# The last expert's way back to its tokens: two d-tiles in turns, two quarters, and a product on GpSimd

## The chip, the core and the metric

The kernel runs on one core of one Trainium2 chip. The metric is the device time of one execution in microseconds, as the median of several runs. TensorE is called PE here, VectorE DVE, ScalarE ACT, GpSimd POOL and SyncE SP.

## What is computed

A decoder trunk of two layers over 512 tokens of width 1024: an mLSTM mixer and a dense SwiGLU, then an HGRN2 mixer and a top-2-of-8 expert SwiGLU. Only the end matters here:

```python
def moe_swiglu(h, router_w, wg, wu, wd):
    ...
    for e in range(N_EXPERTS):
        y = y + gates[:, e:e + 1] * swiglu(t, wg[e], wu[e], wd[e])
    ...
        x = x + gate2 * y
    return rmsnorm(x, final_norm_w)
```

The final norm needs the sum of squares of each token's whole row, so no output row is ready before the last expert's whole row has been added.

## The kernel before

**Work and order.** Every expert gets up to 152 of the tokens (`CAP`). Weights are cut into blocks of 128 x 128; eight blocks are a slot. For every slot, ACT rounds the raw slot to a high half (`whi`) and DVE subtracts that to get the low half (`wlo`); there are five buffers of each, so the high half of a slot can be made only when PE is through with the slot five before it. A block is two matmuls (`mm2`): the high half against both halves of the activations (304 columns), the low half against the high half (152 columns). All engines run strictly in the order in which the program issues; the order is written by hand.

`Weights.get` (lines 254 to 275) is called for every block. Where a block is the first of a slot s, it issues, in this order, the low half of slot s+2 on DVE, the high half of slot s+3 on ACT, then the tasks that are due at s, and only then come the slot's matmuls. `W.at(n, f)` makes f due n slots later; `W.flush` issues all that is left.

**The experts** (`experts`, lines 1597 to 1786). An expert has eleven gate-and-up steps of 16 blocks (`act` makes the hidden activations `hb` from each in five tasks, one slot apart) and a down product of eight d-tiles of eleven blocks (f = 0 to 10, one for each hidden tile). For the last expert the down product is the last thing that PE streams. Before it `W.flush` issues the tasks of the last hidden tiles at once. `down` (lines 1678 to 1722) treats a finished d-tile in tasks: b0 scales one half out of PSUM (ACT), b1 adds the other (DVE, two instructions), b2 transposes the result (PE), and at every fourth d-tile b3 copies the four transposed tiles out. They are due one, two, three and four slots later:

```python
            for i, g in enumerate((b0, b1, b2) + ((b3,) if dd == 3 else ())):
                W.at(i + 1, g)
```

The last expert's first half (d-tiles 0 to 3) goes to memory (`YL`) by two DMAs from POOL (lines 1718 and 1719). Its second half (d-tiles 4 to 7) stays on the chip as four tiles of high and low halves (`last_y`). `add` fetches the rows of the earlier experts for 128 tokens by an indirect DMA from POOL and adds them on DVE (`xt<-yg`), three and four slots later.

**The finish** (`finish`, lines 1798 to 1833). POOL gathers `YL` for four groups of 128 tokens (`yl`). DVE adds each to the residual `xt` and multiplies by the norm's weights (`o<-xt,fw`), ACT sums the squares. Then for each group PE spreads the second half over the tokens by four matmuls with the selection matrix `sel` (`la`, 512 columns), DVE adds, ACT squares; DVE computes 1/sqrt in eight small instructions for two groups at a time (`fv`, `fsy`, `fsa`), DVE and ACT scale the row, and SP sends it out:

```python
            f0(0), f0(1), f0(2), f1(0), f0(3), f2(0), f2(1), f1(1), f2(2), f2(3)
```

Of the kernel before, what the change touches and what calls it, by code (L numbers as in the profile page):

```python
# [21 lines left out]
P = 128  # L22
D = 1024
T = 512
# [60 lines left out]


# [321 lines left out]
class Kernel:  # L408
# [1099 lines left out]
    def moe(self, out, stop):  # L1508
        nc, tc = self.nc, self.tc
        V, S = nc.vector, nc.scalar  # L1510
        with ExitStack() as ctx:
# [28 lines left out]
            g, r, n_over = self.experts(*pools, xt, pick, lambda: rest(*slots))  # L1540
            experts.close()
            self.finish(xt, g, r)
# [54 lines left out]
    def experts(self, xp, hp, wk, xt, pick, rest):  # L1597
# [80 lines left out]
        def down(e, d, yp):  # L1678
# [3 lines left out]
            final = (e, j) == (NE - 1, 1)  # L1682
# [24 lines left out]
            def b3():  # L1707
                if final:
                    for q, n in enumerate((P, R2)):
                        hi, lo = (self.xp.tile([P, T], F32R, name=f"ly{x}{q}", tag="x")[:n] for x in "hl")  # L1710
                        S.activation(hi, tp[q], AF.Copy)
                        V.tensor_sub(lo, tp[q], hi.bitcast(F32))
                        self.last_y += [(q, hi), (q, lo)]
                    return
                for q in range(2):
                    S.activation(yt[q][:, j], tp[q], AF.Copy)
                to, r0 = (self.YL, 0) if e == NE - 1 else (self.Y[j], e * CAP)
# [6 lines left out]
        self.last_y = []  # L1724
# [27 lines left out]
        for kind, e, i in moe_steps():  # L1752
# [21 lines left out]
            else:  # L1774
                if e == NE - 1 and i == 0:
                    W.flush()
                if e == NE - 1 and i in adds[1]:
                    n = len(adds[0]) + adds[1].index(i)
                    add(n % 4, n // 4)
                yp = self.ps(f"yd{e}{i}", (P, 2, CAP))  # L1780
                for f in range(ET):
                    self.mm2(yp, W.get(b), hs[e, f], f == 0, f == ET - 1)
                    b += 1
                down(e, i, yp)
        W.flush()
        return g, r, n_over
# [11 lines left out]
    def finish(self, xt, g, r):  # L1798

        nc, tc = self.nc, self.tc  # L1800
        V, S = nc.vector, nc.scalar
        with tc.tile_pool(name="fin", bufs=4) as fp:
            ssq = fp.tile([P, 2, NC], F32, name="zs", bufs=1)
            zr = fp.tile([P, NC], F32, name="zr", bufs=1)
            o = [fp.tile([P, 2, 512], F32, name=f"o{i}", tag="o") for i in range(NC)]
            ys = [self.xp.tile([P, T], F32, name=f"yl{i}", tag="x") for i in range(NC)]
            for i, y in enumerate(ys):
                nc.gpsimd.indirect_dma_start(out=y, out_offset=None, in_=self.YL,
                                             in_offset=bass.IndirectOffsetOnAxis(ap=r["last"][:, 0, i:i + 1], axis=0))
            for i, y in enumerate(ys):  # L1810
                V.scalar_tensor_tensor(xt[i][0], y, g["last"][:, 0, i:i + 1], xt[i][0], op0=OP.mult, op1=OP.add)
                S.activation(y, xt[i][0], AF.Square, accum_out=ssq[:, 0, i:i + 1])
                V.tensor_mul(o[i][:, 0], xt[i][0], self.fw[:, 0])
            V.tensor_scalar(zr, ssq[:, 0], 1.0 / D, EPS, op0=OP.mult, op1=OP.add)

            def f0(i):
                ps = self.ps(f"la{i}")
                for n, (q, y) in enumerate(self.last_y):
                    nc.tensor.matmul(ps, self.sel[q][:, i * P:(i + 1) * P], y, start=n == 0, stop=n == 3)
                V.scalar_tensor_tensor(xt[i][1], ps, g["last"][:, 0, i:i + 1], xt[i][1], op0=OP.mult, op1=OP.add)  # L1820
                S.activation(o[i][:, 1], xt[i][1], AF.Square, accum_out=ssq[:, 1, i:i + 1])

            rs = {}

            def f1(n):
                v = fp.tile([P, 2], F32, name=f"fv{n}", tag="fv")
                V.scalar_tensor_tensor(v, ssq[:, 1, 2 * n:2 * n + 2], 1.0 / D, zr[:, 2 * n:2 * n + 2], op0=OP.mult, op1=OP.add)
# [50 lines left out]
def _pack(inp):  # L1878
# [17 lines left out]
    moe = np.concatenate([gu, dn], 1).reshape(NE * MB // 8, 8, P, P).transpose(0, 2, 1, 3)  # L1896
# [35 lines left out]
```

## Time and profile before

| | us |
|---|---|
| median of three runs | 1565.17 |
| lowest and highest run | 1562.8 and 1565.18 |
| the profiled execution, device time | 1557.43 |
| its span, first to last instruction | 1555.7 |
| PE busy in the span | 1492.9 |
| DVE busy in the span | 1089.2 |
| ACT busy in the span | 845.3 |
| POOL busy in the span | 133.3 |

The profile is of one execution, which was shorter than the timed ones; times on its axis are microseconds from the start of its span. A busy PE is not a PE at its peak, since matmuls are pipelined. The views used are the page, the busy time by stretch, the timelines of single engines and the rows of one source line. Nearly every instruction is recorded under line 337, that of a helper, so operations are told by the names of what they write and read.

### The profile page before, as it was taken

Reading aid. Unit: us, or ns where it says so; the run is one execution under the profiler, and the core shown is the slowest. Engines: PE = TensorE matmul, PEld = TensorE weight load, DVE = VectorE, ACT = ScalarE, POOL = GpSimd, SP = SyncE. Lnnn points to the kernel's source line nnn. Section 1 sums busy time; section 2 is a strip of 40 time slices with the busy share of each in tenths; the row PEclk is TensorE's granted clock in tenths of the full one; section 3 lists DMA queues with packets and bytes.
Section 4 is the critical chain, followed back from the end, with each engine's and each line's share of the span. In section 5 each row is a group of like instructions: output and inputs, shape, how many; then the busy total and the mean of one; then the engine's idle time right before and its main releaser. Section 6 shows DMA issues by size and latency. Waiting matters only on the chain.

```text
span 1555.7 us, 23596 instructions
## 1 busy us (share of the span) xinstructions
PE 1492.9 (96%) x8955; PEld 1306.8 (84%) x8955; DVE 1089.2 (70%) x1991; ACT 845.3 (54%) x1561; POOL 133.3 (9%) x215
## 2 busy tenths in 40 slices
PE   4989999999999999999999999999999999999996
PEld 3867777888888888688888876899999999999994
DVE  6885774645445555595977744787878878787896
ACT  5566433422212322365656543687786868777763
POOL 0041000000000000310000020501010010101051
PEclk9999999999999999999999999999999999999997
DMA  9462551455455553543102152588687877878792
GB/s 374 167 202 75 196 191 54 156 197 200 157 183 187 193 191 120 186 152 109 55 28 82 55 187 108 194 280 301 249 284 276 277 274 256 300 251 278 275 335 91
DMA packets 80902, 300.47 MB, mean 193 GB/s; under 512 B 8084, under 2 KB 8132, under 8 KB 79760
## 3 DMA queue, kind: packets, MB, share of 16 engines
q1 hardware_dynamic: 68608, 263.21, 47.8%
q0 software_dynamic: 12176, 35.70, 6.9%
q8 instruction: 72, 1.18, 0.3%
q14 instruction: 46, 0.38, 0.1%
HBM read 280.78 MB, written 18.09 MB: 192 GB/s over the span
## 4 chain that ended last, share of the span: by engine, by line
PE 86%; DVE 7%; ACT 3%; DMA 2%; issue 2%; DVEq 0%; SPq 0%; ACTq 0%
PE gu L337 21%; PE yd L337 11%; PE fd L337 8%; PE fgp L337 7%; PE fup L337 7%; PE hh L337 4%; PE al L337 3%; PE hv L337 3%; PE h_out L337 3%; PE m_g L337 3%; PE m_out L337 2%; PE hg L337 2%; PE o L337 2%; PE v L337 1%; PE f_in L337 1%
## 5 line engine op out<-in xcount | busy, mean ns | idle before, releaser
L337 DVE TENSOR_TENSOR wlo<-raw,whi 128x1024 fp32r<-128x1024 f32 x403 | 489.7, 1222 | 101.7 <-ACT whi L337 99.8
L337 ACT ACTIVATE whi<-raw 128x1024 fp32r<-128x1024 f32 x403 | 422.1, 1055 | 169.0 <-DMA raw<-in_w 35.9
L337 PE MATMUL gu<-x,whi 128*128 128x304 f32 x1408 | 358.7, 344 | 1.4 <-DVE x L337 1.0
L337 PE MATMUL gu<-x,wlo 128*128 128x152 f32 x1408 | 327.8, 233 | 0.6 <-issue 0.6
L337 PEld LDWEIGHTS gu<-x,wlo 128*128 128x128 f32 x1408 | 269.1, 191 | 0.7 <-issue 0.4
L337 PEld LDWEIGHTS gu<-x,whi 128*128 128x128 f32 x1408 | 264.4, 188 | 1.9 <-DVE x L337 1.1
L337 PE MATMUL yd<-hb,whi 128*128 128x304 f32 x704 | 181.4, 346 | 1.3 <-DVE hb L337 1.3
L337 PE MATMUL yd<-hb,wlo 128*128 128x152 f32 x704 | 164.2, 233 | 0.0
L337 PEld LDWEIGHTS yd<-hb,wlo 128*128 128x128 f32 x704 | 134.6, 191 | 0.0
L337 PEld LDWEIGHTS yd<-hb,whi 128*128 128x128 f32 x704 | 132.3, 188 | 1.5 <-DVE hb L337 1.5
L337 DVE SCALAR_TENSOR_TENSOR ar<-ar,cond 128x1024 f32<-128x1024 f32 x80 | 98.7, 1237 | 2.8 <-DMA ar<-in_ada 2.7
L337 ACT ACTIVATE fhi<-fg 128x512 fp32r<-128x512 f32 x22 | 13.9, 633 | 114.3 <-DVE fg L337 114.3
L337 DVE TENSOR_TENSOR fg<-fg,fup 128x512 f32<-128x512 f32 x20 | 13.8, 688 | 82.7 <-PE fup L337 82.7
L337 PE MATMUL fd<-fhi,whi 128*128 128x512 f32 x176 | 69.6, 396 | 0.0
L337 PE MATMUL fd<-flo,whi 128*128 128x512 f32 x176 | 69.6, 396 | 0.0
L337 PE MATMUL fd<-fhi,wlo 128*128 128x512 f32 x176 | 69.6, 396 | 0.0
L337 ACT ACTIVATE t<-gu 128x152 f32<-128x152 f32 x176 | 48.2, 289 | 35.9 <-PE gu L337 34.3
L337 PE MATMUL fgp<-lo,whi 128*128 128x512 f32 x160 | 62.3, 389 | 0.0
L337 PE MATMUL fgp<-hi,whi 128*128 128x512 f32 x160 | 62.2, 389 | 0.0
L337 PE MATMUL fgp<-hi,wlo 128*128 128x512 f32 x160 | 62.2, 389 | 0.0
L337 PE MATMUL fup<-hi,whi 128*128 128x512 f32 x160 | 62.2, 389 | 0.0
L337 PE MATMUL fup<-lo,whi 128*128 128x512 f32 x160 | 62.2, 389 | 0.0
(410 smaller groups left out, 2990.1 us busy)
## 6 DMA issues: line engine op xcount, KB each, us to landing
raw<-in_moe SPq DMA_DIRECT2D x125, 1024.0 KB, 5.6
raw<-in_w SPq DMA_DIRECT2D x69, 1024.0 KB, 5.2
ar<-in_ada SPq DMA_DIRECT2D x80, 512.0 KB, 4.4
ad<-in_ada SPq DMA_DIRECT2D x8, 1024.0 KB, 15.2
XG<-zero POOLq DMA_DIRECT2D x18, 256.0 KB
xr<-XG POOLq DMA_DIRECT2D x28, 152.0 KB
raw<-in_moe SPq DMA_DIRECT2D x8, 512.0 KB, 3.4
Y<-yt POOLq DMA_DIRECT2D x14, 256.0 KB
```

The source lines that it names most:

```text
L337: r = f(*args, **kw)
```

## The change

- The eleven slots of the last down product are stored once more in the order `LAST`: d-tiles 0 and 1 in turns, eight blocks of each, then three of each; d-tiles 2 to 7 follow one by one.
- In the last expert every task of a d-tile is due at the next slot, in one go (b0, b1, b2 and what follows).
- The first half's gathers are issued right behind its DMAs to `YL`; the additions and squares of the first two token groups (`first`) are due four slots later.
- The second half is treated in quarters of 256 columns: the first quarter's high and low halves are made at d-tile 5, its matmuls (`share`) for groups 0 and 1 are issued behind the last block and those for 2 and 3 behind the last transposes; its additions and squares (`join`) stand in the finish, ahead of the second quarter's.
- The products with the norm's weights move from DVE to POOL.

```diff
+LAST = [(d, f) for f0, f1 in ((0, KT), (KT, ET)) for d in range(2) for f in range(f0, f1)] + \
+    [(d, f) for d in range(2, KT) for f in range(ET)]
...
-            base = (e - 1) * MB // 8 + 2 * ET
+            base = (e - 1) * MB // 8 + 2 * ET if e < NE else NE * MB // 8
...
-                    for q, n in enumerate((P, R2)):
-                        hi, lo = (self.xp.tile([P, T], F32R, name=f"ly{x}{q}", tag="x")[:n] for x in "hl")
-                        S.activation(hi, tp[q], AF.Copy)
-                        V.tensor_sub(lo, tp[q], hi.bitcast(F32))
-                        self.last_y += [(q, hi), (q, lo)]
+                    c = slice((dd - 1) * P, (dd + 1) * P)
+                    for q, n in enumerate((P, R2)):
+                        t = self.xp.tile([P, 2, 256], F32R, name=f"ly{q}{d}", tag="x")
+                        hi, lo = t[:n, 0], t[:n, 1]
+                        S.activation(hi, tp[q][:, c], AF.Copy)
+                        V.tensor_sub(lo, tp[q][:, c], hi.bitcast(F32))
+                        last_y[d // 2 - 2].extend(((q, hi), (q, lo)))
...
+                if last:
+                    for i in range(NC):
+                        t = self.xp.tile([P, T], F32, name=f"yl{i}", tag="x")
+                        nc.gpsimd.indirect_dma_start(out=t, out_offset=None, in_=self.YL,
+                                                     in_offset=bass.IndirectOffsetOnAxis(ap=r["last"][:, 0, i:i + 1], axis=0))
+                        late[i] = t
+                    for i in range(2):
+                        W.at(4, lambda i=i: first(i, late[i]))
+            def b4():
+                share(0, 2), share(0, 3)
-            for i, g in enumerate((b0, b1, b2) + ((b3,) if dd == 3 else ())):
-                W.at(i + 1, g)
+            gs = (b0, b1, b2) + ((b4,) if final and dd == 3 else ()) + ((b3,) if dd == 3 or (final and dd == 1) else ())
+            for i, task in enumerate(gs):
+                W.at(1 if last else i + 1, task)
...
+        def first(i, t):
+            V.scalar_tensor_tensor(xt[i][0], t, g["last"][:, 0, i:i + 1], xt[i][0], op0=OP.mult, op1=OP.add)
+            S.activation(t, xt[i][0], AF.Square, accum_out=self.ssq3[:, 0, i:i + 1])
+        def share(n, i):
+            if i % 2 == 0:
+                ps = self.ps(f"la{n}{i}").rearrange("p (i c) -> p i c", i=2)
+                parts_of[n, i], parts_of[n, i + 1] = ps[:, 0], ps[:, 1]
+            for m, (q, y) in enumerate(last_y[n]):
+                nc.tensor.matmul(parts_of[n, i], self.sel[q][:, i * P:(i + 1) * P], y, start=m == 0, stop=m == 3)
+        def join(n, i):
+            x = xt[i][1][:, n * 256:n * 256 + 256]
+            V.scalar_tensor_tensor(x, parts_of[n, i], g["last"][:, 0, i:i + 1], x, op0=OP.mult, op1=OP.add)
+            S.activation(late["sq"][:, :256], x, AF.Square, accum_out=self.ssq3[:, 1 + n, i:i + 1])
+        def final():
+            for i in (2, 3):
+                first(i, late[i])
+            for i in range(NC):
+                join(0, i)
+            yield
+            for i in range(NC):
+                share(1, i)
+                join(1, i)
+                yield
...
+        e, acc = NE - 1, {0: yp}
+        for d, f in LAST:
+            if d not in acc:
+                if d in adds[1]:
+                    n = len(adds[0]) + adds[1].index(d)
+                    add(n % 4, n // 4)
+                acc[d] = self.ps(f"yd{e}{d}", (P, 2, CAP))
+            self.mm2(acc[d], W.get(b), hs[e, f], f == 0, f == ET - 1)
+            b += 1
+            if f == ET - 1:
+                down(e, d, acc[d])
+        share(0, 0), share(0, 1)
         W.flush()
...
-                V.tensor_mul(o[i][:, 0], xt[i][0], self.fw[:, 0])
...
+            next(final)
+            for i in range(NC):
+                nc.gpsimd.tensor_mul(o[i][:, 0], xt[i][0], self.fw[:, 0])
+            V.tensor_add(zr, ssq[:, 0], ssq[:, 1])
+            V.tensor_scalar(zr, zr, 1.0 / D, EPS, op0=OP.mult, op1=OP.add)
...
             def f0(i):
-                ps = self.ps(f"la{i}")
-                for n, (q, y) in enumerate(self.last_y):
-                    nc.tensor.matmul(ps, self.sel[q][:, i * P:(i + 1) * P], y, start=n == 0, stop=n == 3)
-                V.scalar_tensor_tensor(xt[i][1], ps, g["last"][:, 0, i:i + 1], xt[i][1], op0=OP.mult, op1=OP.add)
-                S.activation(o[i][:, 1], xt[i][1], AF.Square, accum_out=ssq[:, 1, i:i + 1])
+                next(final)
```

## Rows read from the trace of the kernel before

**Rows 1.** The page's chain of work that ended last, by engine: shares of the span.

```profile
PE 86%; DVE 7%; ACT 3%; DMA 2%; issue 2%; DVEq 0%; SPq 0%; ACTq 0%
```

**Rows 2.** Busy time by stretch: from:to in us, its length, busy us and instruction count of PE, PEld, DVE, ACT, POOL, then granted clock, DMA share, GB/s. The start of the last down product.

```profile
1507.00:1511.00 4.00, 2.81 (x22) 2.61 (x21) 4.00 (x12) 1.91 (x6) 0.87 (x1) 1.00 1.03 409
```

**Rows 3.** Timeline of PE (start, length, operation; idle time before it and its releaser in brackets) in the last down product: its first matmul, the matmul of the first d-tile's eleventh block, the 25th block, and the last matmul.

```profile
1507.06 0.35 PE L337 MATMUL yd<-hb,whi 128*128 128x304 f32 x1
...
1511.11 0.41 PE L337 MATMUL yd<-hb,whi 128*128 128x304 f32 x1 [1.30 <-DVE hb L337]
...
1514.69 0.34 PE L337 MATMUL yd<-hb,whi 128*128 128x304 f32 x1
...
1531.30 0.24 PE L337 MATMUL yd<-hb,wlo 128*128 128x152 f32 x1
```

**Rows 4.** Timeline of DVE in the same stretch, in its order: hidden activation, four low halves of weights, the first d-tile's eviction, an addition of an earlier expert.

```profile
1510.75 0.30 DVE L337 TENSOR_TENSOR hb<-t,hb 128x152 fp32r<-128x152 f32 x1
...
1510.98 4.62 DVE L337 TENSOR_TENSOR wlo<-raw,whi 128x1024 fp32r<-128x1024 f32 x4
...
1515.52 0.49 DVE L337 SCALAR_TENSOR_TENSOR y<-yd,mod,y 128x128 f32<-128x128 f32 x2
...
1517.07 0.74 DVE L337 SCALAR_TENSOR_TENSOR xt<-yg,gelse,xt 128x512 f32<-128x512 f32 x1
```

**Rows 5.** Timeline of ACT: three high halves of weights, a later one with its wait, and the second copy of the first four transposed d-tiles.

```profile
1510.43 2.94 ACT L337 ACTIVATE whi<-raw 128x1024 fp32r<-128x1024 f32 x3
...
1516.83 1.06 ACT L337 ACTIVATE whi<-raw 128x1024 fp32r<-128x1024 f32 x1 [0.90 <-PE yd L337]
...
1525.79 0.27 ACT L337 ACTIVATE yt<-yq 96x128 f32<-96x128 f32 x1
```

**Rows 6.** Timeline of POOL: the first and the last of the four indirect gathers of the last expert's rows.

```profile
1530.56 1.01 POOL L1808 DMA_INDIRECT yl<-YL,rlast  x1 [3.06 <-DVE y L337]
...
1534.39 0.95 POOL L1808 DMA_INDIRECT yl<-YL,rlast  x1 [0.30 <-DVE lyl L337]
```

**Rows 7.** Busy time by stretch, columns as in group 2: the DMA of the gathers, and that of the output.

```profile
1532.00:1538.00 6.00, 4.75 (x10) 2.10 (x10) 4.98 (x9) 2.53 (x7) 2.73 (x3) 0.69 0.66 179
...
1547.00:1552.30 5.30, 0.00 (x0) 0.00 (x0) 2.30 (x6) 0.72 (x1) 0.00 (x0) 0.50 1.01 395
```

**Rows 8.** Timelines of ACT, DVE and the SP queue behind the last down product (ACT's four rows of squares are shown by one).

```profile
1531.63 0.39 ACT L337 ACTIVATE y<-yd,mod 128x152 f32<-128x152 f32 x1 [2.38 <-PE yd L337]
...
1532.05 0.50 DVE L337 SCALAR_TENSOR_TENSOR y<-yd,mod,y 128x128 f32<-128x128 f32 x2 [2.26 <-ACT y L337]
...
1533.45 0.69 DVE L337 TENSOR_TENSOR lyl<-yp,lyh 128x512 fp32r<-128x512 f32 x1 [0.90 <-ACT lyh L337]
...
1534.65 0.73 DVE L337 SCALAR_TENSOR_TENSOR xt<-yl,glast,xt 128x512 f32<-128x512 f32 x1
...
1535.42 0.69 DVE L337 TENSOR_TENSOR o<-xt,fw 128x512 f32<-128x512 f32 x1
...
1540.42 2.06 DVE L337 SCALAR_TENSOR_TENSOR xt<-la,glast,xt 128x512 f32<-128x512 f32 x3
...
1541.85 0.63 ACT L337 ACTIVATE o<-xt 128x512 f32<-128x512 f32 x1
...
1542.61 0.16 DVE L337 SCALAR_TENSOR_TENSOR fv<-zs,zr 128x2 f32<-128x2 f32 x1
...
1546.20 3.59 SPq L1796 DMA_DIRECT2D out<-o  x4
```

**Rows 9.** Timeline of PE: two of the sixteen matmuls that spread the last expert's rows over the tokens (third and last), and two pairs of neighbours of the output projection, the first pair inside a stretch at a granted clock of 0.5, the second behind it.

```profile
1534.82 0.79 PE L337 MATMUL la<-lyh,sel 24*128 24x512 f32 x1
...
1542.31 0.62 PE L337 MATMUL la<-lyl,sel 24*128 24x512 f32 x1
...
911.51 0.63 PE L337 MATMUL h_out<-hlo,whi 128*128 128x512 f32 x1
...
911.94 0.63 PE L337 MATMUL h_out<-hhi,wlo 128*128 128x512 f32 x1
...
913.40 0.39 PE L337 MATMUL h_out<-hhi,whi 128*128 128x512 f32 x1
...
913.63 0.40 PE L337 MATMUL h_out<-hlo,whi 128*128 128x512 f32 x1
```

**Rows 10.** Busy time by stretch, columns as in group 2: two stretches without matmuls, what came a little later, and the end.

```profile
185.00:188.30 3.30, 0.00 (x0) 0.00 (x0) 2.83 (x7) 2.59 (x5) 0.00 (x0) 1.00 0.59 187
...
189.50:192.50 3.00, 3.00 (x9) 2.31 (x8) 3.00 (x6) 0.00 (x0) 0.00 (x0) 0.50 0.71 218
...
907.50:909.30 1.80, 0.04 (x1) 0.00 (x0) 0.03 (x1) 1.67 (x6) 0.00 (x0) 1.00 0.91 330
...
909.70:912.90 3.20, 2.99 (x8) 2.26 (x8) 2.05 (x3) 2.08 (x4) 0.54 (x1) 0.50 0.45 149
...
1534.30:1542.90 8.60, 8.60 (x15) 3.57 (x15) 8.24 (x15) 4.60 (x13) 0.95 (x1) 0.50 0.28 80
```

**Rows 11.** POOL's elementwise products of 128x512 (durations min/median/max in ns), a DVE instruction that ran beside the first of them, and the page's row for all of that DVE instruction's kind (busy us, mean ns).

```profile
L884 POOL TENSOR_TENSOR dt<-dt,cst_m x8: 1266/1300/2268, 85.5 to 128.5; 128x512 f32<-128x512 f32 x8
...
85.76 2.13 DVE L337 SCALAR_TENSOR_TENSOR ar<-ar,cond 128x1024 f32<-128x1024 f32 x1
...
L337 DVE SCALAR_TENSOR_TENSOR ar<-ar,cond 128x1024 f32<-128x1024 f32 x80 | 98.7, 1237 | 2.8 <-DMA ar<-in_ada 2.7
```

More of the change, by code (lines that the diff above doesn't have):

```diff
@@ L1539, in moe @@
             pick, rest, *slots = self.route(rp, lps, xt)
-            g, r, n_over = self.experts(*pools, xt, pick, lambda: rest(*slots))
+            g, r, n_over, final = self.experts(*pools, xt, pick, lambda: rest(*slots))
             experts.close()
-            self.finish(xt, g, r)
+            self.finish(xt, final)
             n = nc.values_load(n_over, min_val=0, max_val=2 * T)
@@ L1681, in down @@
             j, dd, cs = d // 4, d % 4, slice((d % 4) * P, (d % 4 + 1) * P)
-            final = (e, j) == (NE - 1, 1)
+            last = e == NE - 1
+            final = last and j == 1
             if dd == 0:
@@ L1776, in experts @@
                     W.flush()
-                if e == NE - 1 and i in adds[1]:
-                    n = len(adds[0]) + adds[1].index(i)
-                    add(n % 4, n // 4)
                 yp = self.ps(f"yd{e}{i}", (P, 2, CAP))
+                if e == NE - 1:
+                    break
                 for f in range(ET):
@@ L1784, in experts @@
                 down(e, i, yp)
+        late["sq"] = self.nrm.tile([P, T], F32, name="sqs", tag="rs", bufs=1)
+        e, acc = NE - 1, {0: yp}
[10 more added lines that the diff above has]
+        share(0, 0), share(0, 1)
         W.flush()
-        return g, r, n_over
+        return g, r, n_over, final()
     def rows_out(self, i, xt, o, rs, on_act):
@@ L1796, in rows_out, with finish @@
         nc.sync.dma_start(self.a["out"][i * P:(i + 1) * P], o.rearrange("p j c -> p (j c)"))
-    def finish(self, xt, g, r):
+    def finish(self, xt, final):
         nc, tc = self.nc, self.tc
@@ L1802, in finish @@
         with tc.tile_pool(name="fin", bufs=4) as fp:
-            ssq = fp.tile([P, 2, NC], F32, name="zs", bufs=1)
+            ssq = self.ssq3
             zr = fp.tile([P, NC], F32, name="zr", bufs=1)
             o = [fp.tile([P, 2, 512], F32, name=f"o{i}", tag="o") for i in range(NC)]
[L1806 to L1812, printed above, removed]
-                V.tensor_mul(o[i][:, 0], xt[i][0], self.fw[:, 0])
-            V.tensor_scalar(zr, ssq[:, 0], 1.0 / D, EPS, op0=OP.mult, op1=OP.add)
-            def f0(i):
-                ps = self.ps(f"la{i}")
-                for n, (q, y) in enumerate(self.last_y):
-                    nc.tensor.matmul(ps, self.sel[q][:, i * P:(i + 1) * P], y, start=n == 0, stop=n == 3)
-                V.scalar_tensor_tensor(xt[i][1], ps, g["last"][:, 0, i:i + 1], xt[i][1], op0=OP.mult, op1=OP.add)
-                S.activation(o[i][:, 1], xt[i][1], AF.Square, accum_out=ssq[:, 1, i:i + 1])
+            next(final)
[3 more added lines that the diff above has]
+            V.tensor_scalar(zr, zr, 1.0 / D, EPS, op0=OP.mult, op1=OP.add)
+            def f0(i):
+                next(final)
             rs = {}
@@ L1826, in f1 @@
                 v = fp.tile([P, 2], F32, name=f"fv{n}", tag="fv")
-                V.scalar_tensor_tensor(v, ssq[:, 1, 2 * n:2 * n + 2], 1.0 / D, zr[:, 2 * n:2 * n + 2], op0=OP.mult, op1=OP.add)
+                V.scalar_tensor_tensor(v, ssq[:, 2, 2 * n:2 * n + 2], 1.0 / D, zr[:, 2 * n:2 * n + 2], op0=OP.mult, op1=OP.add)
                 rs[n] = self.rsqrt(v, fp, "fs")
@@ L1895, in _pack @@
     dn = blk(f("moe_w_down")[0]).transpose(0, 3, 1, 2, 4).reshape(NE, -1, P, P)
-    moe = np.concatenate([gu, dn], 1).reshape(NE * MB // 8, 8, P, P).transpose(0, 2, 1, 3)
+    more = np.stack([dn[NE - 1, d * ET + n] for d, n in LAST])
+    moe = np.concatenate([np.concatenate([gu, dn], 1).reshape(-1, P, P), more]).reshape(-1, 8, P, P).transpose(0, 2, 1, 3)
     col = lambda v: v.reshape(-1, P).T
```

6 lines of the change are left out of this document (4 added, 2 removed).

## The prediction

> **What bounds the kernel now.** I read four views in this order. The chain of work that ended last says that PE carries 86% of the span [rows 1], so what moves PE's last matmul moves the end. The stretch table and PE's timeline then show how the last down product begins: it starts at 1507.06, runs at one block in 0.25 us, and waits once, for the hidden activation of its eleventh block (f = 10), which starts at 1511.11 where ten blocks put it at 1509.6; it ends at 1531.54 [rows 3]. DVE is busy for the whole of those four microseconds [rows 2], so that wait is DVE's backlog and not PE's own work. DVE's timeline shows that the backlog goes on: behind the last hidden activation (to 1511.05) stand four low halves of weights in one go, to 1515.60, and the first d-tile's eviction comes only then, although PE finished that tile near 1511.4 [rows 4]. Before, this lag is harmless: the transposes are issued three slots after the tile, and PE streams on. Last I read the finish: from PE's last block to the first output DMA it takes 1546.20 - 1531.54 = 14.7 us, mostly DVE in one chain [rows 8], and then the four output DMAs run at full rate for 5.3 us [rows 7], so the end follows the first of them.
>
> **Part by part.** I number the slots of the down product 0 to 10, 2.0 us each, and put everything on the axis of the profile.
>
> *Two d-tiles in turns.* f = 8 to 10 now come as blocks 16 to 18, which are due at 1507.06 + 16 x 0.25 = 1511.1. The hidden activations are there by then. But block 16 is also the first of slot 2, whose low half DVE starts at 1510.98 and ends at 1512.2 (4.62 us for four, 1.14 apart) [rows 4]. So a wait for `wlo` takes the place of the wait for `hb`: slot 2 starts near 1512.1, where it started at 1514.69 - 2.0 = 1512.7 [rows 3]. **Gain 0.6**, not 1.5. The slots' copy in the new order is loaded by as many DMAs on SP as before, of the same sizes: nothing there.
>
> *All tasks due at the next slot.* Tiles 0 and 1 both end in slot 2, and both their transposes are now issued ahead of slot 3 on PE, which runs in order. PE is ready at 1514.1. DVE has first to finish the low halves of slots 2 to 5 (1515.60), then an addition of an earlier expert (0.67 apart; `add` for tile 1 is called after 8 blocks instead of 11, so its first addition falls due one slot earlier), then two evictions of 0.45 each [rows 4]: 1517.1. Slot 3 starts at 1517.2 instead of 1514.69. **Loss 2.5**, with PE idle for 2.6 us. What is queued behind: the whole of slot 3, and through it ACT, whose high half for slot 8 may start only when PE leaves slot 3; a wait of that kind is there already, 0.90 [rows 5].
>
> *Slots 3 to 7.* Slot 4 at 1519.2, tile 2's transpose is in time, slot 5 at 1521.5, tile 3's two transposes wait 0.2, slot 6 at 1523.9. Tile 4 ends one block ahead of slot 7. ACT has before its b0 the two copies of tiles 0 to 3 (behind the transposes, to 1524.8) and the last high half (0.98 each [rows 5], to 1525.8); then b0 0.4 and b1 0.5 [rows 8], so the transpose runs at 1526.85 where PE is ready at 1525.9: **0.9 lost**, and 0.3 in the small waits. Slot 7 starts at 1527.1, slot 9 ends at 1533.3.
>
> *The first half sooner.* The copies end at 1524.8 instead of 1526.06 [rows 5]. From there to the first gather it took 4.5 us before [rows 6], two DMAs and their landing; so the gathers start at 1529.3, 1.28 apart [rows 6] (on POOL only the products stand behind them), and the second is issued by 1531.5. When a gather's data is there no wait shows. Bounds: 0.6 us behind the issue, where the DMA starts to move, and 2.7, where the last issue ends at 1535.34 and the DMA goes quiet by 1538 [rows 6, 7]. I take 2.1, near the upper end because that row holds the whole transfer: 1533.6. Now the additions `first` for groups 0 and 1 are due at slot 10, and they were registered before tile 6's tasks. So ahead of slot 10 stand, in order: addition 0.74, square 0.8 with its accumulator, b0 0.4, b1 0.5 [rows 8], the transposes: 1536.05, where PE is ready at 1533.3. **Loss 2.7** (2.3 to 3.3 by those bounds). Slot 10 runs from 1536.3 to 1538.3; before, PE ended at 1531.5. Sum so far: **+6.8**.
>
> *The finish, at the same clock.* Off DVE's chain go two of the four additions of `yl` (2 x 0.67), the four products (4 x 0.68), half the width of two `lyl` (0.6) and of three additions of `la` (2.06 to 1.2) [rows 8]; on it come four `join` of the first quarter (4 x 0.4, estimated between the 0.22 of 128 columns that half a b1 takes and the 0.67 of 512 columns), one small addition (0.2), and a wait of about 1.0 for ACT, whose squares (0.66 apart [rows 8], 0.45 at 256 columns, estimated in the same way) must end before `zr`. -1.3 - 2.7 - 0.6 - 0.9 + 1.6 + 0.2 + 1.0 = -2.7, and the transposes of tiles 5 and 6, gone from behind the last block, give 0.4 more: **-3.1**. The products on POOL cost nothing as long as they end before ACT scales the rows some 9 us into the finish; four take 4 x 1.3 = 5.2 to 4 x 2.3 = 9.1 [rows 11].
>
> A DVE instruction beside such a product took 2.13 us against a mean of 1.24 [rows 11]. So the two remaining `first` additions can each be held up by one product: nothing to 2 x 1.3 = 2.6 us. I take nothing, because at the clock that I expect (next part) DVE waits for PE there anyway; the upper end is rival 5. The Trainium skill, on the page "SBUF — State Buffer", section "Who interferes with whom", says that a DVE instruction with two SBUF inputs contends with a GpSimd instruction that reads SBUF and that the later one blocks fully. The trace agrees in direction with that 2.13; by the rule the sum would take the upper end, 2.6 more (rival 5), since `first` reads two SBUF operands and `join` only one.
>
> *The clock.* Without it the sum is 6.8 - 3.1 = +3.7. But PE now stands idle twice for about 2.6 us. The rows show what followed such gaps: after 3.30 idle us PE ran at a granted 0.50 (1.2 GHz) from 189.5 on, after 1.80 from 909.7 on, for some 3 us each [rows 10]; the 1.3 us wait of now left it at 1.00 [rows 2, 3]. At 1.2 GHz matmuls were 0.43 apart against 0.23 [rows 9], so three microseconds lose about 1.5. First gap: 1.1 of it reaches the end, the rest falls on the small waits. Second gap: slot 10 loses 1.0 of the 1.7 that it would lose in full, since part of the slow stretch lies in the gap. The finish ran at 0.50 before as well [rows 10]: a `la` matmul took 0.576 (13 steps in 7.49 us [rows 9]); 256 columns at 1.2 GHz less make 0.36, so a `share` of four takes 1.45 instead of some 0.6 at 2.4 GHz. Two of them stand ahead of the last transposes: 1.7 if all is slow, 0.9 taken. 1.1 + 1.0 + 0.9 = **+3.0**, between 0 and 4.5.
>
> **Sum: +6.7.** On the profiled execution's own time: span 1555.7 to 1562.4, device time 1557.43 to 1564.1. The median of the runs shown is 1565.17, 7.7 above that execution; I carry the difference over: 1571.9. The output DMAs stay 5.3 us behind the first of them and change nothing.
>
> **The rivals.** (1) *The waits don't bite, faster:* DVE comes to the evictions before PE comes to slot 3. Then only -0.6 and the shorter finish are left: 1565.17 - 3.7 = 1561.5. It decides at 1514.1: DVE's work before the second eviction must be 3.1 us, not the 6.1 that its own rows give. For it speaks that DVE is the lighter engine over the whole span; against it, rows 2 and 4. Chance 0.10. (2) *Only the first wait:* the gathers land 2.5 us sooner, or tile 6's eviction doesn't wait for the squares. Then +6.8 becomes +4.1, and the sum is +1.0, or +2.1 with one fall of the clock: 1566.2 to 1567.3. Chance 0.16. (3) *No fall of the clock:* +3.7, 1568.9. Against it, both gaps of that size in the rows. Chance 0.18. (4) *The change doesn't do what it says,* since the wait for `hb` only turns into one for `wlo`: that is in my sum already and worth 0.9. (5) *The products hold up DVE:* both remaining `first` additions wait for a whole product, and PE is not what DVE waits for next: +6.7 + 2.6 = +9.3, 1574.5. For it the 2.13; against it, that the products may be half over by then. Chance 0.10.
>
> **The numbers.** The forecast, +6.7, has 0.44; worse than +10 has 0.02. A measurement of this kernel tells about 0.2%, 3.1 us, from no change. Faster by more: rival 1, 0.10. Within: rival 2 and a corner of rival 3, 0.18. Slower by more: 0.72. The range goes from rival 2's lower value, 1566.2, to 1575.8: all tail at 1.2 GHz (+1.5) and most of the port's 2.6.
>
> **What would show it.** Right: PE idle for about 2.6 us near 1514 with the release by DVE's `y`, and again near 1533 behind an addition of `yl`; the last block of `yd` near 1538 to 1541; the first output DMA 11 to 14 us behind it; a granted clock below 1.00 between 1515 and 1531. Wrong: no PE wait over 1 us between the first and the last `yd`, or `yl` additions that end before 1531, or a full clock throughout.

## The result, and the profile after

| | before | after |
|---|---|---|
| median (us) | 1565.18 | 1576.0 |
| lowest and highest run | 1562.8 and 1566.53 | 1574.59 and 1577.8 |
| profiled execution, device time | 1557.43 | 1575.41 |

Ratio 1.0089, 95% interval 1.0064 to 1.0114: slower, as forecast, but by 10.8 us between the medians where the sum said 6.7. The three waits that the sum was made of are all there; the third, ahead of slot 10, and the clock cost more than their terms, and the finish gave nothing back.

Two profiled executions can't be laid on each other by their axes. The four low halves behind the last hidden activation start at 1515.37, where they started at 1510.98 [rows 4]: 4.4 us are lost ahead of the change. Most of that arises near 1003 us, in unchanged code. The busy time by stretch (columns as in group 2), first of before:

```profile
1003.00:1007.00 4.00, 4.00 (x34) 4.00 (x33) 3.09 (x6) 4.00 (x10) 0.60 (x1) 1.00 1.03 407
```

and of after:

```profile
1003.00:1007.00 4.00, 3.70 (x17) 3.59 (x16) 2.58 (x4) 3.55 (x8) 0.97 (x2) 0.50 1.02 411
```

Half as many matmuls in the same time, at half the granted clock. So from here on I count from the start of those four low halves, and call the time from there to the first output DMA the **end part**. It took 35.2 us before (1546.20 - 1510.98 [rows 4, 8]) and takes 48.3 after.

The chain of work that ended last is still PE's [rows 1]:

```profile
PE 85%; DVE 6%; DMA 3%; ACT 3%; issue 2%; POOL 0%; DVEq 0%; SPq 0%; another core or an unknown queue 0%; POOLq 0%; ACTq 0%
```

Those are shares of the whole span. Ahead of slot 10 the chain leaves PE, as the prediction's "first half sooner" had it: from 1531.99 to 1544.87 it runs through the two DMAs to `YL`, a gather, the second addition of `yl` and an eviction. The gather is its longest step there (start, us):

```profile
1537.62 3.93 DMA yl<-YL,rlast
```

PE's timeline after, the waits and the rows around them (start, length, operation, idle time before it and its releaser):

```profile
1511.67 0.34 PE L340 MATMUL yd<-hb,whi 128*128 128x304 f32 x1
...
1516.64 0.34 PE L340 MATMUL yd<-hb,wlo 128*128 128x152 f32 x1 [0.61 <-DVE wlo L340]
...
1520.97 0.89 PE L340 MATMUL yp<-cst_c,y 128*128 128x128 f32 x2 [2.24 <-DVE y L340]
1521.51 0.60 PE L340 MATMUL yd<-hb,whi 128*128 128x304 f32 x1
...
1528.08 0.34 PE L340 MATMUL yd<-hb,whi 128*128 128x304 f32 x1
...
1533.89 0.33 PE L340 MATMUL yp<-cst_c,y 128*128 128x128 f32 x1 [0.65 <-DVE y L340]
...
1544.87 0.33 PE L340 MATMUL yp<-cst_c,y 128*128 128x128 f32 x1 [4.29 <-DVE y L340]
...
1545.06 0.59 PE L340 MATMUL yd<-hb,whi 128*128 128x304 f32 x1
...
1548.63 0.23 PE L340 MATMUL yd<-hb,wlo 128*128 128x152 f32 x1
...
1556.81 2.97 PE L340 MATMUL la<-ly,sel 128*128 128x256 f32 x8 [3.64 <-DVE xt L340]
...
1560.36 1.52 PE L340 MATMUL la<-ly,sel 128*128 128x256 f32 x4 [0.58 <-DVE xt L340]
```

Inside the down product the one wait of before, 1.30 for `hb` [rows 3], has become four: for `wlo` in slot 2 and for the evictions ahead of slots 3, 7 and 10. In the finish stand two, 3.64 and 0.58; before had three small ones behind its last block, of 0.48, 0.58 and 0.22. The last block ends at 1548.86, 33.5 us behind the four low halves; before 20.6. DVE's timeline beside it:

```profile
1515.37 4.62 DVE L340 TENSOR_TENSOR wlo<-raw,whi 128x1024 fp32r<-128x1024 f32 x4
1519.91 0.74 DVE L340 SCALAR_TENSOR_TENSOR xt<-yg,gelse,xt 128x512 f32<-128x512 f32 x1
1520.57 0.90 DVE L340 SCALAR_TENSOR_TENSOR y<-yd,mod,y 128x128 f32<-128x128 f32 x4
...
1539.96 0.75 DVE L340 SCALAR_TENSOR_TENSOR xt<-yl,glast,xt 128x512 f32<-128x512 f32 x1 [0.27 <-DMA yl<-YL,rlast]
1541.58 1.82 DVE L340 SCALAR_TENSOR_TENSOR xt<-yl,glast,xt 128x512 f32<-128x512 f32 x1 [0.86 <-DMA yl<-YL,rlast]
1544.46 0.50 DVE L340 SCALAR_TENSOR_TENSOR y<-yd,mod,y 128x128 f32<-128x128 f32 x2 [1.06 <-ACT y L340]
...
1553.13 1.64 DVE L340 SCALAR_TENSOR_TENSOR xt<-la,glast,xt 128x256 f32<-128x256 f32 x4
```

The first three lines are the queue that the prediction read out of [rows 4]: four low halves, an addition, two evictions, and only then the transposes. The next three are slot 10's: both additions wait for the gathers' data, and the second takes 1.82 us where such a one took 0.73 to 0.75 [rows 4, 8]. POOL's timeline shows what ran beside it:

```profile
1531.99 0.59 POOL L1724 DMA_DIRECT2D YL<-yt  x1 [19.72 <-ACT yt L340]
...
1536.31 1.01 POOL L1729 DMA_INDIRECT yl<-YL,rlast  x1 [3.01 <-issue]
1537.62 0.97 POOL L1729 DMA_INDIRECT yl<-YL,rlast  x1 [0.30 <-issue]
...
1541.55 1.29 POOL L1873 TENSOR_TENSOR o<-xt,fw 128x512 f32<-128x512 f32 x1
...
1552.62 2.96 POOL L1873 TENSOR_TENSOR o<-xt,fw 128x512 f32<-128x512 f32 x2 [7.88 <-DVE xt L340]
```

ACT's timeline answers to [rows 5]: the high half that waited 0.90 for PE waits 5.21, and the copies of the first half, ahead of POOL's two DMAs, end at 1531.84.

```profile
1525.41 1.06 ACT L340 ACTIVATE whi<-raw 128x1024 fp32r<-128x1024 f32 x1 [5.21 <-PE yd L340]
...
1531.58 0.26 ACT L340 ACTIVATE yt<-yq 96x128 f32<-96x128 f32 x1
```

In POOL's rows the first product with the norm's weights starts at 1541.55, as soon as the first group's row is added, 0.03 us ahead of the second addition. The stretches of the end (columns as in group 2):

```profile
1517.00:1521.00 4.00, 1.76 (x15) 1.58 (x14) 4.00 (x7) 3.21 (x5) 0.00 (x0) 1.00 0.49 153
1521.00:1528.70 7.70, 7.62 (x36) 7.43 (x37) 5.99 (x11) 1.33 (x2) 0.00 (x0) 0.56 0.01 3
1528.70:1531.50 2.80, 2.80 (x24) 2.64 (x23) 1.56 (x4) 1.86 (x3) 0.00 (x0) 1.00 0.00 0
...
1540.50:1544.80 4.30, 0.08 (x2) 0.00 (x0) 2.38 (x4) 1.72 (x5) 3.59 (x3) 1.00 0.37 138
1544.80:1548.90 4.10, 4.03 (x20) 4.02 (x20) 0.16 (x2) 0.00 (x0) 0.00 (x0) 0.58 0.00 0
1548.90:1563.60 14.70, 8.76 (x34) 5.84 (x33) 8.71 (x26) 6.98 (x25) 2.96 (x2) 0.72 0.00 1
```

Behind each long PE wait stands a stretch near a granted 0.5 (1.2 GHz): 1521 to 1528, and nearly all of slot 10. The SP queue gives the first output and so the finish's length, 1563.63 - 1548.86 = 14.8 us, as long as before (14.7):

```profile
1563.63 3.73 SPq L1861 DMA_DIRECT2D out<-o  x4
```

### The profile page after: what moved, and what is told of

Its sections match the earlier page's. It is cut to its first block, busy times and chain, and to the rows that moved or that the text cites. A ratio compares the mean times of both kernels' runs of the same rounds, so it can differ in the third digit from the quotient of the medians.

```text
span 1573.7 us, 23653 instructions
## 1 busy us (share of the span) xinstructions
PE 1501.2 (95%) x8971; PEld 1316.0 (84%) x8971; DVE 1088.9 (69%) x1994; ACT 847.1 (54%) x1571; POOL 138.1 (9%) x219
## 4 chain that ended last, share of the span: by engine, by line
PE 85%; DVE 6%; DMA 3%; ACT 3%; issue 2%; POOL 0%; DVEq 0%; SPq 0%; another core or an unknown queue 0%; POOLq 0%; ACTq 0%
PE gu L340 22%; PE yd L340 10%; PE fd L340 8%; PE fgp L340 7%; PE fup L340 7%; PE hh L340 4%; PE al L340 3%; PE hv L340 3%; PE h_out L340 3%; PE m_g L340 3%; PE m_out L340 2%; PE o L340 2%; PE hg L340 2%; PE v L340 1%; PE h_first L340 1%
## 5 line engine op out<-in xcount | busy, mean ns | idle before, releaser
L340 PE MATMUL yd<-hb,whi 128*128 128x304 f32 x704 | 185.9, 352 | 0.0
L340 DVE TENSOR_TENSOR fg<-fg,fup 128x512 f32<-128x512 f32 x20 | 13.8, 688 | 82.7 <-PE fup L340 82.7
L340 PE MATMUL fup<-hi,wlo 128*128 128x512 f32 x160 | 62.2, 389 | 0.0
```

Of the source, the lines that this page charges most:

```text
L340: r = f(*args, **kw)
```

## The experiments

My theory: the loss is made by the three PE waits of the down product, by the clock that falls behind them, and by a finish in which a shared PSUM buffer, which the prediction had not seen, lets `share` and `join` take turns. One part at a time is put back, then several together. Profiled executions, in us (`down`: first to last block of the last down product; `to last block` and `end part` count from the four low halves; `tail`: first output to the end of the span):

| run | down | to last block | finish | end part | tail | first PE wait over 1.2 us, and the clock behind it |
|---|---|---|---|---|---|---|
| before | 24.5 | 20.6 | 14.7 | 35.2 | 9.5 | 1.30 `hb`, stays full |
| before again | 28.8 | 23.4 | 16.0 | 39.5 | 9.5 | 1.34 and 1.30 `hb`, falls |
| after | 37.2 | 33.5 | 14.8 | 48.3 | 10.0 | 2.24 `y`, falls |
| after again | 36.6 | 32.4 | 16.0 | 48.5 | 10.3 | 2.24 `y`, falls |
| transposes later | 35.6 | 30.9 | 16.0 | 46.9 | 10.4 | 1.61 `wlo`, stays full; 2.42 `y`, falls |
| additions in the finish | 29.9 | 26.2 | 17.8 | 44.0 | 10.3 | 2.24 `y`, falls |
| products on DVE | 32.3 | 29.6 | 17.1 | 46.7 | 10.2 | 2.19 `y`, stays full |
| a buffer for each `share` | 37.1 | 32.2 | 13.8 | 46.1 | 9.8 | 1.81 `wlo`, stays full; 2.23 `y`, falls |
| new order alone | 28.7 | 23.1 | 14.7 | 37.8 | 9.5 | 2.47 `wlo`, falls |
| tasks staggered, and three more | 28.2 | 23.2 | 15.7 | 38.9 | 9.8 | 1.86 `wlo`, falls |
| the same, finish in pairs | 29.8 | 24.8 | 10.9 | 35.6 | 12.5 | 1.91 `wlo`, falls |
| before, additions later | 24.1 | 21.4 | 14.7 | 36.0 | 9.5 | none, stays full |
| both of the last two | 28.4 | 25.4 | 10.9 | 36.3 | 12.9 | 2.19 `y`, falls |

In the two rows with additions later the four low halves start sooner against PE, since four additions ahead of them are gone; there `down` is the column to compare, not the two that count from the low halves.

**Before once more** (b_again), unchanged.

> The kernel before, unchanged, for a second profile. Its first profiled execution took 1557.43 us, 7.7 below its median, and up to 1000 us the two profiles (before, change) differ by 0.6 us, from 1047 on by 4.7 us, although the code there is the same. Theory: the executions differ by a wait near 1000 us, in the scatter of the rows to the experts, and not at the end; then this profile has its end part (from the four low halves of weights behind the last hidden activation to the first output DMA) at 35.2 us again, within 0.3, whatever its whole time is. Rival: the difference lies in the end part itself; then it is over 38 us here.

PE's timeline, and a stretch (columns as in group 2):

```profile
1506.87 0.41 PE L337 MATMUL yd<-hb,whi 128*128 128x304 f32 x1 [1.34 <-DVE hb L337]
1508.65 0.62 PE L337 MATMUL yd<-hb,whi 128*128 128x304 f32 x1 [1.30 <-DVE hb L337]
```

```profile
1509.00:1514.00 5.00, 5.00 (x23) 5.00 (x23) 5.00 (x7) 3.25 (x5) 0.00 (x0) 0.50 0.35 120
```

Here PE waits twice for `hb`, and the clock falls: 23 matmuls in 5 us. Up to the last block that makes 2.9 us more than in the first profile. The finish is 1.4 longer for another reason: the last gather takes 1.80 us to issue instead of 0.95 [rows 6], and DVE waits for its rows. POOL's and DVE's timelines:

```profile
1534.82 1.80 POOL L1808 DMA_INDIRECT yl<-YL,rlast  x1 [0.30 <-DVE lyl L337]
```

```profile
1540.56 0.75 DVE L337 SCALAR_TENSOR_TENSOR xt<-yl,glast,xt 128x512 f32<-128x512 f32 x1 [1.26 <-DMA yl<-YL,rlast]
```

So the rival came: the end part of the kernel before is 35.2 or 39.5 us, and the change adds 13.0 or 8.8 to it. The sum was made on the shorter.

**Tiles 0's and 1's transposes three slots later** (e1_late_t).

```diff
-                W.at(1 if last else i + 1, task)
+                W.at(3 if last and d < 2 and task is b2 else 1 if last else i + 1, task)
```

> With the change, but the transposes of d-tiles 0 and 1 are due three slots later, as before, instead of at the next slot; nothing else differs. The end part (from the four low halves behind the last hidden activation to the first output DMA) takes 48.3 us with the change. Theory: PE's first wait (2.24 us for DVE's y) and the fall of the clock behind it (slots 3 to 6 are 2.7 us longer than at full clock) both go: end part about 43.3, granted clock 1.00 up to the wait of slot 10. Rival: DVE's backlog only moves the wait to slot 5, and the clock falls there: end part 47 to 48.5.

PE's timeline:

```profile
1511.31 0.34 PE L340 MATMUL yd<-hb,wlo 128*128 128x152 f32 x1 [1.61 <-DVE wlo L340]
1520.06 0.33 PE L340 MATMUL yp<-cst_c,y 128*128 128x128 f32 x1 [2.42 <-DVE y L340]
```

The theory missed, and the rival came nearly to its size, 46.9. The wait ahead of slot 3 is gone and stands as 2.42 us ahead of slot 5 instead: DVE has no pause from the four low halves on, so PE, let through earlier, comes to tile 2's eviction before DVE does. Here the wait for a full queue moved; it didn't end.

**The four gathered additions in the finish** (e2_first_late).

```diff
-                    for i in range(2):
-                        W.at(4, lambda i=i: first(i, late[i]))
...
-            for i in (2, 3):
+            for i in range(NC):
                 first(i, late[i])
```

> With the change, but all four additions of the gathered rows stand in the finish (none is due ahead of slot 10). Theory: PE's wait ahead of slot 10 (4.29 us) falls to under 0.3, slot 10 runs at full clock (2.0 us instead of 3.5), and the finish takes up two additions and two squares, 1.3 to 2.6 us: end part 48.3 - 4.2 - 1.4 + 2.0 = 44.7, between 43.5 and 46. Rival: the additions and squares set the finish anyway, as the gathered rows come late: no more than 1 us less.

The end part, 44.0, is within the expected range. The wait ahead of slot 10 shrinks to 0.16, and the down product is 7.3 us shorter than after's: 4.1 of that is the wait, 1.6 the slow slot behind it, and the rest comes from the first fall of the clock, which lasted 3.4 us here and 6.8 in after. The finish is 3.0 longer. DVE's and POOL's timelines there show one more price:

```profile
1545.06 2.72 DVE L340 SCALAR_TENSOR_TENSOR xt<-yl,glast,xt 128x512 f32<-128x512 f32 x4
...
1550.58 0.84 DVE L340 TENSOR_TENSOR zr<-ssq 128x4 f32<-128x4 f32 x1 [1.24 <-ACT sqs L340]
1551.45 1.19 DVE L340 TENSOR_SCALAR zr<-zr 128x4 f32<-128x4 f32 x1
```

```profile
1545.94 6.68 POOL L1871 TENSOR_TENSOR o<-xt,fw 128x512 f32<-128x512 f32 x4 [5.91 <-DVE xt L340]
```

Two instructions on four columns, 0.16 and 0.17 us in after, take 0.84 and 1.19 while POOL is at its products.

**A PSUM buffer for each `share`** (e4_banks).

```diff
-            if i % 2 == 0:
-                ps = self.ps(f"la{n}{i}").rearrange("p (i c) -> p i c", i=2)
-                parts_of[n, i], parts_of[n, i + 1] = ps[:, 0], ps[:, 1]
+            parts_of[n, i] = self.ps(f"la{n}{i}", (P, 256))
```

> With the change, but each spread (share) has a PSUM buffer of its own, instead of two groups in the halves of one. Theory: PE's waits of 3.64 and 0.58 us for DVE's additions inside the finish come from the shared buffer; without them the second quarter's matmuls are done before the squares of the first end, DVE's three additions stand back to back behind zr, and the first output DMA comes 2 to 3 us sooner: end part 45.3 to 46.3. Rival: ACT's chain of squares sets the finish, and the wait of PE hides behind it: less than 0.7 us.

PE's timeline of the finish, behind the last block:

```profile
1547.50 2.88 PE L340 MATMUL la<-ly,sel 128*128 128x256 f32 x8
1550.32 0.47 PE L340 MATMUL yp<-cst_c,y 128*128 128x128 f32 x1
1550.65 8.73 PE L340 MATMUL la<-ly,sel 128*128 128x256 f32 x24
```

No wait is left in it. Its finish, all at 1.2 GHz, took 13.8 us against 16.0 of after again, all at 1.2 GHz too: the shared buffer cost 2.2, of the 2 to 3 expected.

**The products back on DVE** (e3_dve_prod), one line in the finish.

```diff
-                nc.gpsimd.tensor_mul(o[i][:, 0], xt[i][0], self.fw[:, 0])
+                V.tensor_mul(o[i][:, 0], xt[i][0], self.fw[:, 0])
```

> With the change, but the four products with the norm's weights are on DVE in the finish again, none on POOL. With the change the second gathered addition, ahead of slot 10, took 1.82 us beside a product on POOL that began 0.03 us before it; the first one took 0.75. Theory: the two hold each other up, so here both additions take 0.75, PE's wait ahead of slot 10 is 1.0 to 1.2 us shorter (4.29 to about 3.2), and the finish pays up to 2.7 us for four products on DVE, less what hides in its wait for the squares (1.2): end part 48.3 - 1.1 + 1.5 = 48.7, within 47.5 and 50. Rival: the addition was long for the arrival of its rows and not for the product: it takes 1.8 again, PE waits 4.3.

DVE's and PE's timelines:

```profile
1539.54 0.75 DVE L340 SCALAR_TENSOR_TENSOR xt<-yl,glast,xt 128x512 f32<-128x512 f32 x1 [0.73 <-DMA yl<-YL,rlast]
```

```profile
1541.76 0.47 PE L340 MATMUL yp<-cst_c,y 128*128 128x128 f32 x1 [3.08 <-DVE y L340]
```

The second addition is back to 0.75, and slot 10's wait is 3.08 instead of 4.29. So the product on POOL costs 1.1 to 1.2 us of PE time there. Between the waits ahead of slots 3 and 7 the down product gained 3 us more, because the clock stayed full behind the 2.19 us wait; so the end part, 46.7, fell below the expected 47.5 to 50. The finish, all at 1.2 GHz, is 1.1 longer than that of after again, which was at 1.2 GHz throughout too: there the move to POOL does help.

**The new order alone** (e5_turns): the kernel before, with the slots' copy and the loop over `LAST`, nothing else.

> The kernel before with only the new order of the last down product (d-tiles 0 and 1 in turns); tasks, finish and products as before. From the four low halves to PE's last block of the product the kernel before takes 20.6 us at full clock (23.4 where the clock fell). Theory: the wait of 1.3 for hb goes, one of 0.6 to 1.0 for wlo comes, nothing else: 19.8 to 20.2. Rival: all of the 1.3 is gained, 19.2 or less; or nothing is, 20.6.

```profile
1513.47 0.50 PE L340 MATMUL yd<-hb,wlo 128*128 128x152 f32 x1 [2.47 <-DVE wlo L340]
```

That is PE's timeline: the wait for `hb` is a wait for `wlo`, as forecast. Slot 2 starts 1.27 us behind the four low halves, so at full clock slot 3 would have started some 0.5 earlier than before's (3.71 behind [rows 3, 4]). The number, 23.1, missed because the clock fell for 6.8 us; against before again, whose clock fell as long, the order gains 0.3 in this one pair of profiles.

**Tasks of tiles 0 to 3 due in steps as before, additions in the finish, own buffers** (c1_stagger).

```diff
-                W.at(1 if last else i + 1, task)
+                W.at(1 if final else i + 1, task)
```

> With the change, but the tasks of d-tiles 0 to 3 are due one, two, three and four slots later as before, all gathered additions stand in the finish, and every spread has a PSUM buffer of its own. Theory: what made the change slower are PE's waits ahead of slots 3 and 10, the two falls of the clock behind them, and the shared buffer; without these PE ends its last block 20 to 21.5 us behind the start of the four low halves (33.5 with the change) and the finish takes 12 to 14 (14.8), so the end part is 32.5 to 35.5, at or under the 35.2 of before. Rival: the quarters, the products on POOL or the gathers cost the time; then it stays over 38.

The waits ahead of slot 3 and in the finish are gone, and that ahead of slot 10 is 0.17: 9.4 us less than after. Both halves missed all the same, and the end part, 38.9, came to the rival's size. The last block came at 23.2 instead of 20 to 21.5: at the `wlo` wait, 1.86 long here, the clock fell for 3.4 us. The finish took 15.7 instead of 12 to 14, and there two of the rival's reasons hold. On DVE's timeline the third addition of `yl` waits 0.80 for its rows, and it and the fourth take 2.62 us beside POOL's products (from 1540.10 on), where the first two took 1.39:

```profile
1541.41 2.62 DVE L340 SCALAR_TENSOR_TENSOR xt<-yl,glast,xt 128x512 f32<-128x512 f32 x2 [0.80 <-DMA yl<-YL,rlast]
```

**The same with the finish in pairs of groups** (c2_pairs): 1/sqrt for groups 0 and 1 ahead of the additions for 2 and 3, products half on POOL and half on DVE.

```diff
+            share(1, 0), share(1, 1)
+            first(0, late[0]), first(1, late[1])
+            yield
+            join(0, 0), join(0, 1), join(1, 0), join(1, 1)
+            yield
+            share(0, 3), share(1, 2), share(1, 3)
...
```

> As c1, and the finish is ordered by pairs of token groups: the additions, spreads and squares of groups 0 and 1 first, then their 1/sqrt, while those of groups 2 and 3 follow; products of 0 and 1 on POOL, of 2 and 3 on DVE where it waits for squares. Theory: PE's last block as in c1, the first output DMA 10 to 11.5 us behind it instead of 14.7 before, the others in time for the output's rate: end part 30.5 to 33, and 3 to 5 us less than the kernel before, a ratio of 0.997 to 0.998. Rival: the gathers' arrival or the half clock of the spreads sets the finish, as before: 13 us or more, no difference that can be measured.

Median 1561.26, kernel before 1559.2, ratio 1.0009 (0.9992 to 1.0026): no difference. The SP queue:

```profile
1549.77 7.09 SPq L1861 DMA_DIRECT2D out<-o  x4
```

The last block came at 24.8 instead of 20 to 21.5, as the clock fell for 6.8 us behind the `wlo` wait. The first output is there 10.9 us behind it, as expected, but the four are issued over 7.1 us instead of 3.6 [rows 8], and the tail is 12.5 instead of 9.5. Finish and tail together: 23.4 against 24.1 and 25.5 of the two executions of before.

**After once more** (after_again), unchanged.

> The changed kernel, unchanged, timed again beside more runs of the kernel before. The kernel before showed 1553 to 1567 us over 25 runs so far, and its end part 35.2 us in one profile and 39.5 in another, where the clock fell at PE's wait for hb. Theory: the change costs its end part, 48.3 against 35.2 to 39.5 us, and 0.5 us at the output: 9.5 to 13.5 us more, a ratio of 1.006 to 1.009. Rival: part of the first comparison's 10.8 us came from runs of before that happened to be long or short; then it is under 8 or over 15.

Median 1571.78 against 1558.22, 13.6 us more, ratio 1.0094 (1.0064 to 1.0124): at the upper end of what was expected. The end part repeats within 0.2 us, with other stretches at 1.2 GHz: behind the 2.24 us wait the clock is down for 3.4 us, where it was 6.8, and from slot 10 on it stays down to the end. The stretch behind that wait (columns as in group 2):

```profile
1513.20:1516.60 3.40, 3.40 (x17) 3.40 (x16) 3.02 (x4) 0.55 (x1) 0.00 (x0) 0.50 0.00 0
```

**The kernel before, four of its additions later** (n1_adds): additions of an earlier expert move from the last gate-and-up steps into the down product.

```diff
-        adds = ((3, 5, 6, 8, 9, 10), (1, 2))
+        adds = ((3, 5, 6, 8), (1, 2, 3, 4))
```

> The kernel before with one line changed: the last two fetches of earlier experts' rows (four additions of 0.67 us on DVE that stand between the last hidden activations) are made at d-tiles 3 and 4 of the last down product instead of at its last two gate steps. Theory: PE's wait at the first d-tile is DVE's backlog, so these four additions set it; without them the last hidden activation is there 1.3 to 2.7 us sooner, PE waits under 0.3 us, the clock doesn't fall, and the span from the four low halves' old place on loses 1.3 us where the clock stayed up before and 4 us where it fell: ratio 0.9975 to 0.999. Rival: the chain of the activation itself (PE, ACT and DVE in turn) sets it and PE waits 1 us or more; no difference.

Median 1556.43, kernel before 1558.22 on the same chip, ratio 0.9991 (0.9975 to 1.0007). PE's timeline has no wait for `hb` or `wlo` at all, and the granted clock stays full to the finish; the down product is 24.1 us, 0.4 less than in the profile where before's clock stayed full and 4.8 less than in the other (expected: 1.3 and 4). The cause of the wait was DVE's queue, and this empties it ahead of the last activations. Its interval still holds no change.

**Both** (n2_adds_pairs): c2_pairs with those additions, and small moves in the finish.

> c2_pairs with those four additions moved as in n1, the additions of the first quarter for groups 0 and 1 ahead of the second quarter's low halves on DVE, and the last row scaled on ACT. Theory: PE waits under 0.5 us for wlo at slot 2 (1.91 in c2_pairs), the clock stays at 1.00 to the last block, which comes 19.5 to 21 us behind the start of the product's first low halves instead of 24.8 there; with c2's finish the kernel is 3.5 to 5.5 us under c2_pairs and 2 to 4 under the kernel before: ratio 0.9975 to 0.9987. Rival: the clock falls all the same, or the moved additions delay the evictions: a ratio within 0.999 to 1.001.

```profile
1520.65 0.33 PE L340 MATMUL yp<-cst_c,y 128*128 128x128 f32 x1 [2.19 <-DVE y L340]
```

Median 1558.69, ratio 1.0006 (0.999 to 1.0022): no difference, as the rival said. In PE's timeline no wait for `wlo` is left, but one of 2.19 ahead of slot 7: tile 4's transposes are due at the next slot, and the moved additions now stand in DVE's queue ahead of its eviction.

## Why the prediction was right in sign and short in size

The median after, 1576.0, lies 0.2 above the upper end of the forecast range, 1575.8; the sum was 4.1 us too small. Of the signs that were to show it, the waits and the clock came. The last block and the first output did not: the block comes 33.5 us behind the four low halves, where 1538 to 1541 on the axis of before is 27 to 30, and the output 14.8 behind the block instead of 11 to 14.

Against its own terms, in the two profiled executions:

| step | forecast | measured | from |
|---|---|---|---|
| ahead of slot 3 | 2.5 | 2.4 | slot 3 starts 6.14 behind the low halves (3.71 before) |
| clock behind that wait | 1.1 | 3.1 | 14 blocks in 6.57 us, at 0.25 they take 3.5 |
| tile 4, small waits | 1.2 | 0.65 | ahead of slot 7 |
| wait ahead of slot 10 | 2.7 | 4.3 | 4.29 |
| clock in slot 10 | 1.0 | 1.6 | slot 10 in 3.80 us, slot 9 in 2.2 at full clock |
| rest of the last block's delay | 0.4 | 0.9 | 12.9 less the lines above |
| finish with its clock | -2.2 | +0.1 | 14.77 against 14.66 |
| output to end | 0 | 0.5 | 10.0 against 9.5 |
| **the change** | **6.7** | **13.6** | |
| ahead of the last product | 0 | 4.4 | other execution, same code |

The forecast's 0.4 is what its 6.8 at the last block holds beside 2.5, 1.2 and 2.7. 13.6 and 4.4 make the 18.0 between the two profiled executions.

**Right:** the wait for `hb` became one for `wlo`; DVE's queue behind the low halves was read to 0.1 us; the second wait stands where it was put, ahead of slot 10 behind an addition of `yl`. "The transposes wait for the queue" is shown by e1, where they go and another wait comes; "slot 10 waits for the gathered additions" by e2, where they go and the wait with them.

**Wrong, the clock's first term.** Three microseconds at 1.2 GHz were taken, from [rows 10], and 1.1 of the 1.5 let through. The stretch lasted 6.8 us in after, and 3.4 in after again, so the term is 3.1 or some 1.6 (by the same time for a block), and it delays the end because the copies of the first half, where the last chain goes on, wait for PE's transposes in slot 6.

**Wrong, the second wait's size.** The copies ended 2.65 us later than forecast on this axis, for the clock, but PE too came to slot 10 2.9 us later, so that adds nothing. From there the first gather came in 4.47 (4.5 taken [rows 5, 6]). What was short is the landing: data was used 2.6 and 3.0 us behind the issue's end, where 2.1 was taken, and the second, which slot 10 waits for, is above the upper bound, 2.7. And the second addition ran beside the first product.

**Wrong, "the products on POOL cost nothing".** The prediction looked for the collision in the finish (rival 5) and kept 0 to 2.6 for it; it came in slot 10, on the path of PE, because a product may start as soon as its own group's row is added. e3 gives its price, 1.2. The Trainium skill, page "SBUF — State Buffer", section "Who interferes with whom", says that a DVE instruction with two SBUF inputs and a GpSimd instruction that reads SBUF lock each other out, the later blocking fully, and that one with a single SBUF input isn't touched outside the two-port modes. The trace agrees in both: 1.82 us for the addition that began 0.03 behind a product, and 0.41 each for the four additions of `la`, whose other input is in PSUM, beside the two products from 1552.62 on, as long as in e3 without a product (1.64 for the four in both). Two rows stay open. In e2 the second instruction on four columns has a single SBUF input and took 1.19 all the same; no row tells whether it ran in a two-port mode. In e1 the second addition began 0.65 us ahead of the product and still took 2.48; POOL was issuing the fourth gather until just before, and no run separates that issue from the product. DVE's and POOL's timelines of e1:

```profile
1533.46 2.48 DVE L340 SCALAR_TENSOR_TENSOR xt<-yl,glast,xt 128x512 f32<-128x512 f32 x1 [0.20 <-DMA yl<-YL,rlast]
```

```profile
1532.37 1.72 POOL L1729 DMA_INDIRECT yl<-YL,rlast  x1 [0.30 <-DVE ly L340]
1534.11 1.27 POOL L1873 TENSOR_TENSOR o<-xt,fw 128x512 f32<-128x512 f32 x1
```

**Wrong, the finish's -3.1.** It was summed as DVE's work. But two groups' `share` lie in the halves of one PSUM buffer, and the program makes the second group's matmuls wait until DVE has read the first's: 3.64 and 0.58 us of PE idle in after. e4 takes the sharing away, and its finish is 2.2 shorter than that of after again, whose waits there were 1.88 and 0.58. With all spreads at 1.2 GHz the prediction's own terms make -3.1 + 1.7 = -1.4; e4, all at 1.2 GHz, is 0.8 under before, so the buffer is most of what was missing. The last groups' chain was of PE and DVE in turns, and a sum over DVE alone couldn't see it.

**The base.** The sum was carried from the profiled execution to the median by a constant. Before again shows that the kernel before can lose 4.3 us in its own end part: 2.9 up to the last block, where its clock falls, and 1.4 in the finish, where a gather comes late. The changed kernel's end part was the same within 0.2 in its two profiles, so what the change adds depends on the execution of before that it is held against. The medians' difference, 10.8, lies between the two that the profiles give, 13.6 and 9.4 (8.8 in the end part and close to 0.6 in the tail); the second measurement gave 13.6. How often each kernel's clock falls in its end part is open: the timed runs have no profile.

## What to carry to other kernels

When an instruction waits for a queue that is full, look for what fills the queue ahead of it: four additions moved to a later step took PE's wait away, while moving PE's own work only moved the wait. An operation given to an idle engine can start in places that you didn't think of, so look up from which point its inputs are ready and who runs then. Before halves of a buffer are shared, check that the writer of the second doesn't wait for the reader of the first.

## What the runs showed of the hardware

- The granted clock fell to 0.50 behind PE waits of 1.3 to 2.5 us in some executions and not in others: after 2.24 us for 6.8 us in one execution of after and for 3.4 in the other, after 2.19 not at all in e3 and for 3.4 in n2, after 1.86 for 3.4 in c1 and after 1.81 not at all in e4, from within the second of two waits, 1.34 and 1.30, for 6.8 in before again, after one of 1.30 not at all in before [rows 2, 3]. No run here tells what decides.
- Where DVE waited for an indirect gather of 128 rows of 2 KB, it used the data 2.6 to 3.2 us behind the end of the issue (after, e1, e3, c1), and once, in before again, 3.9.
- DVE's smallest instructions on SBUF, 0.16 to 0.17 us, took 0.84 and 1.19 beside POOL's products, although they hold four columns. They lost 0.68 and 1.02, the `yl` addition of 512 columns lost 1.07 beside one product: in these three rows the loss doesn't go by DVE's own size.
